# Turns of statistics, operand sums, attention loads and filter taps in a two-block transformer layer on one core

## The chip, the core and the metric

One core of a Trainium2 chip runs the whole program in one launch. The metric is the device time of one execution in microseconds. Every time below comes from one profiled execution of the kernel before, or from the unprofiled runs where that is said.

## The reference, cut to what matters

Two layers follow each other on 1,024 positions of width 1,024, in float32.

```python
# first block
h = rms_norm(x, norm_g);  u = h @ w_in
v_c, b_c, c_c, z_c, q, k, v, z_a, gate_logits = split(u)
y_a = (b_c * conv3(c_c * v_c) * silu(z_c)) @ w_conv_out
q, k = rms_norm(q) , rms_norm(k)                 # per head of 64
o   = window_attention(q, k, v, sinks) * silu(z_a)   # 16 heads, window 128
y_b = o @ w_attn_out
x   = x + (sigmoid(g_a) * y_a + sigmoid(g_b) * y_b) @ w_out
# second block
x = x + mixer(rms_norm(x)) ; x = x + cross_attention(rms_norm(x), mem)
u = rms_norm(x) @ w_up                           # 2 * 2816 columns
u = conv_b + w0 * u[t-2] + w1 * u[t-1] + w2 * u[t]
x = x + (silu(u[:, :2816]) * u[:, 2816:]) @ w_down
```

## The kernel before, in words

Activations lie with features on the 128 partitions and positions along the row. The 1,024 positions are two halves of 512 (`h` 0 and 1); a width of 1,024 is eight tiles (`kt`). A float32 product is made from three matmuls on high and low parts: ScalarE copies the high part, VectorE (sometimes GpSimd) subtracts it to get the low part. A **dense** page (`dense`, lines 381 to 383 for its matmuls) is 24 matmuls of 128x512 for one half. A **pair** of pages (`wino`, matmuls at lines 410 to 412) covers two pages and both halves with seven products of 12 matmuls instead of eight. Its operands besides the pages are the halves themselves and four sums of halves, T1 to T4, which `sums` (lines 447 to 487) makes from normalised tiles: subtractions in place, then a high and a low part for each of four tiles. T1 is wanted in the second product of the first pair, T2 in the third, T3 in the fifth, T4 in the seventh.

Everything else is woven between matmuls by hand. `tick()` is one **turn**: it sends the pending low parts of weights, one step of the pair being prepared, and one step of every generator in `side`. A dense page calls it halfway and at its end, a pair after every product. Each engine runs its instructions in the order in which they were written, so what a turn emits sits behind all that was emitted earlier on that engine. Loads and stores issued on `nc.sync` go through SyncE's queue (SP), those on `nc.gpsimd` through GpSimd's, also each in written order. Small tiles come from rings: 64 half tiles (`hp`), 8 temporaries (`tp`), two raw weight pages (`wr`), and a region reopened from stage to stage (`pg`, `hq`).

The places that the change touches:

- `x_thread` (lines 687 to 703) normalises one half. Each of eight tiles is written to a temporary, split into high and low, and stored to memory (`hraw`).
- `hT_sums` (lines 835 to 855) waits until both halves are normalised and the keys and values are stored, reopens the region, loads all 16 stored tiles back in three turns and a side generator, and then runs `sums`. Meanwhile TensorE works through four dense `z` pages; then come two `z` pairs, four `q` pairs, four `gb` pairs, eight times two convolution pairs and four `ga` pairs.
- `q_out` (lines 863 to 891) evacuates each quarter of a `q` pair: a square, a high and a low part. Its `stats`, run in the next turn, stores the two parts, sums the squares over each head with four small matmuls (line 882) and raises the mean to a power on GpSimd.
- `att_in` (lines 1022 to 1038) issues on GpSimd all loads of one group of heads and one half: two of keys, eight of queries, four of `z`, and for the first group two of values. Both groups of half 0 are issued before the convolution output pages `co` begin; the others are issued at units 9 and 17.
- `attention` (line 1155 on) takes 32 units, one a turn, after three empty turns, alongside `co`. In a turn come the values of three units ago, the finish and transpose of earlier ones (lines 1103 and 1123), and the scores of the new unit (line 1073), whose masked tile `pr` is first filled by GpSimd (line 1066) in the four units that have no block before them.
- `Up` (line 1728 on) evacuates an up page of the feed-forward layer: a copy to `u`, the last tap and the bias as a scaled copy on ScalarE, then two taps on VectorE (lines 1746 and 1747), all in the same turn. The first three of 22 page couples are plain dense pages, and `sums` for the other 19 runs beside them.

Of the kernel before, what the change touches and what calls it, by code (L numbers as in the profile page):

```python
# [17 lines left out]
HT = 512  # L18
# [98 lines left out]
def _body(es, tc, nc, wp, vec, xT, memT, gk2, pw, cst, out, dbg):  # L117
# [328 lines left out]
    def sums(t, X, hts):  # L446


        at = {"T1": (0, 0), "T2": (4, 1), "T3": (0, 1), "T4": (4, 0)}
        his, los = {}, {}  # L450

        def u(name, k):
            return t[at[name][0] + k, at[name][1]]

        def hi(name, k):
            his[name, k] = hts[name](name, F32R)
            S.copy(his[name, k], u(name, k))

        def lo(name, k):
            los[name, k] = hts[name](name, F32R)  # L460
            V.tensor_tensor(los[name, k], u(name, k), f(his[name, k]), ALU.subtract)  # L461
            if k == 3:
                X[name] = [(his[name, i], los[name, i]) for i in range(4)]

        for k in range(4):
            V.tensor_tensor(u("T1", k), u("T3", k), u("T1", k), ALU.subtract)
            V.tensor_tensor(u("T3", k), u("T3", k), u("T2", k), ALU.subtract)
            hi("T1", k)
            yield
        for k in range(4):  # L470
            V.tensor_tensor(u("T2", k), u("T2", k), u("T1", k), ALU.subtract)
            lo("T1", k)
            hi("T2", k)
            yield
        for k in range(4):
            lo("T2", k)
            V.tensor_tensor(u("T4", k), u("T4", k), u("T2", k), ALU.subtract)
            hi("T3", k)
            yield
        for k in range(4):  # L480
            lo("T3", k)
            hi("T4", k)
            if k:
                lo("T4", k - 1)
            yield
        lo("T4", 3)
# [184 lines left out]
    hraw = {}  # L671
# [15 lines left out]
    def x_thread(h):  # L687
# [7 lines left out]
        for kt in range(KT):  # L695
            t = tp("xn")
            V.scalar_tensor_tensor(t, xs[kt][h], col("norm_g", kt), R, ALU.mult, ALU.mult)
            hT[kt][h] = [None, None]
            sp.add(t, hT[kt][h], "xn")
            hraw[kt, h] = dram("hraw")  # L700
            nc.sync.dma_start(hraw[kt, h], t)
            if kt % 2:
                yield
# [130 lines left out]

    def hT_sums():
        while None in [x[1] for x in hT] or len(kd) < 8 or len(vd) < 4:
            yield
        reopen("q1pool", 16)
        t = {}
        order = [(kt, h) for k in range(4) for kt, h in ((k, 0), (k, 1), (k + 4, 1))] + [(k, 0) for k in range(4, 8)]  # L840

        def loads():
            for i, (kt, h) in enumerate(order):
                t[kt, h] = (hp if (kt < 4) == (h == 0) or kt == 7 else hq)("ht")
                nc.sync.dma_start(t[kt, h], hraw[kt, h])
                if i in (3, 7, 9, 11, 13):
                    yield

        g = loads()
        for _ in range(3):  # L850
            next(g)
            yield
        side.append(g)
        yield from sums(t, XB, {"T1": hp, "T2": hp, "T3": hq, "T4": hq})

# [10 lines left out]
    def q_out(p, j, h, o):  # L866
# [10 lines left out]
        def stats():  # L877
            for dst, src in zip(qd[p, j, h], (qh, ql)):
                nc.sync.dma_start(dst, f(src))
# [8 lines left out]
            return  # L888
            yield
# [132 lines left out]
    def att_in(p, h):  # L1022

        if h == 0:
            kp[p] = pg("kh", F32R), pg("kl", F32R)
        for i in range(2):
            nc.gpsimd.dma_start(f(kp[p][i][:, h * HT:(h + 1) * HT]), kd[p, h, i])
        for j in range(4):
            qT[p, j, h] = hp("qh", F32R), hp("ql", F32R)
            for i in range(2):  # L1030
                nc.gpsimd.dma_start(f(qT[p, j, h][i]), qd[p, j, h][i])
            if j == 1 and p == 0:
                vv[h] = pg("vh", F32R, (P, 4, 256)), pg("vl", F32R, (P, 4, 256))
                for i in range(2):
                    nc.gpsimd.dma_start(f(vv[h][i]), vd[h, i])
        for j in range(4):
            oT[p][j][h] = hp("o")
            nc.gpsimd.dma_start(oT[p][j][h], zd[p, j, h])

    class Unit:  # L1040
# [17 lines left out]
        def scores(self):  # L1058
# [6 lines left out]
            if n == 0:  # L1065
                G.memset(pr, -1e30)
# [87 lines left out]
    def attention():  # L1154
# [4 lines left out]
        for _ in range(3):  # L1159
            yield  # L1160
        for i in range(n + 3):
# [15 lines left out]
            if i in (9, 17):  # L1177
                att_in(i // 16, 1)
# [19 lines left out]
    for p in range(2):  # L1198
        att_in(p, 0)
    gate_in(gin, gad, 0, 0)  # L1200
    while None in [yc[c][0] for c in range(KT)]:
# [524 lines left out]
    class Up:  # L1726
# [5 lines left out]
        def tile(self, w, h):  # L1732
            u = self.u[w, h] = tp("u", shape=(P, HT + 2))
            if h == 0:
                G.memset(u[:, 0:2], 0.0)  # L1735
            return u[:, 2:]

        def conv(self, w, h):
            base = (NFF if w else 0) + self.ft
            w0, w1, w2 = (col("ffn_w", k * 44 + base) for k in range(3))  # L1740
# [4 lines left out]
            S.activation(a, u[:, 2:], AF.Identity, bias=col("ffn_b", base), scale=w2)  # L1745
            V.scalar_tensor_tensor(a, u[:, 1:HT + 1], w1, a, ALU.mult, ALU.add)  # L1746
# [11 lines left out]
        def plain(self, w):  # L1758
            def run(o, h):
                S.copy(self.tile(w, h), o)  # L1760
                self.conv(w, h)
                if w == 0:
                    side.append(self.gate_later(h))
                else:
                    self.out(h)
            return run

        def gate_later(self, h):
            yield
            self.gate(h)  # L1770
# [269 lines left out]
```

## Time and profile before

| What | us |
|---|---|
| unprofiled runs: median of 3 (lowest to highest) | 2487.8 (2484.42 to 2496.45) |
| profiled execution, its own time | 2496.53 |
| its span, first to last instruction | 2494.7 |
| TensorE busy in the span | 2394.4 |
| VectorE / ScalarE / GpSimd busy | 1471.7 / 1010.2 / 608.5 |

Busy time of an engine is the sum of its instructions without overlap; the span less that is the time in which the engine had nothing running. The profiled execution's time is 1.8 us above its span. [...]

### The profile page before, as it was taken

The numbers are of one execution on the slowest core, as the hardware profiler recorded it, in microseconds if no ns is written. First come the engines' busy times: TensorE is split into PE (matmuls) and PEld (weight loads), VectorE is DVE, ScalarE is ACT, GpSimd is POOL, SyncE is SP. The second block draws the span as 40 slices with busy tenths as digits, with TensorE's granted clock in tenths as the row PEclk, the third lists the DMA queues.
The fourth block names the chain that finished last, engine by engine and source line by source line (L and its number), as shares of the span: only waits on it lengthen the run. The fifth ranks groups of instructions, "written<-read, shape, count | busy, mean of one in ns | idle before, by whom it ended". The sixth has DMA issues, their size and how long they took to land. (4 is left out here: it accounts for less than half of the span.)

```text
span 2494.7 us, 30966 instructions
## 1 busy us (share of the span) xinstructions
PE 2394.4 (96%) x11550; PEld 1959.4 (79%) x11550; DVE 1471.7 (59%) x2303; ACT 1010.2 (40%) x1871; POOL 608.5 (24%) x629
## 2 busy tenths in 40 slices
PE   8988899999997889999999999999999999999998
PEld 7866688888885677887887888888878888878887
DVE  6642336666634778646435556455677878874335
ACT  5433343333343666334512334344455555562212
POOL 3234432333313555022001020001204233310003
PEclk9999999999998999999999999999999999999999
DMA  4622231211246533641100235322522222244322
GB/s 164 249 93 102 102 110 60 80 65 68 68 136 231 190 133 104 211 145 61 51 28 28 76 115 165 120 70 89 169 65 80 81 96 77 76 140 151 101 78 89
DMA packets 106231, 269.17 MB, mean 108 GB/s; under 512 B 12352, under 2 KB 14816, under 8 KB 106080
## 3 DMA queue, kind: packets, MB, share of 16 engines
q1 hardware_dynamic: 98544, 244.11, 29.1%
q0 software_dynamic: 6992, 22.55, 2.5%
q8 instruction: 91, 1.49, 0.2%
q10 hardware_dynamic: 544, 0.52, 0.1%
q14 instruction: 60, 0.49, 0.1%
HBM read 205.28 MB, written 61.87 MB: 107 GB/s over the span
## 5 line engine op out<-in xcount | busy, mean ns | idle before, releaser
L411 PE MATMUL pss<-T,wsh 128*128 128x512 f32 x588 | 232.4, 395 | 9.2 <-DVE T L461 9.2
L410 PE MATMUL pss<-T,wsh 128*128 128x512 f32 x588 | 236.6, 402 | 2.0 <-DVE cb L991 1.2
L345 DVE TENSOR_TENSOR wl<-wr,wh 128x1024 fp32r<-128x1024 f32 (+1 forms) x147 | 177.3, 1206 | 99.2 <-ACT wh L281 99.1
L412 PE MATMUL pss<-T,wsl 128*128 128x512 f32 x588 | 232.6, 396 | 0.0
L566 POOL TENSOR_TENSOR sq<-sq,sq 128x512 f32<-128x512 f32 (+1 forms) x58 | 70.9, 1223 | 610.2 <-ACT sq L562 609.1
L298 POOL TENSOR_TENSOR ws<-wr 128x512 f32<-128x512 f32 x49 | 70.8, 1445 | 586.4 <-DMA wr<-in_wp_dram 468.3
L330 DVE TENSOR_TENSOR wsl<-ws,wsh 128x512 fp32r<-128x512 f32 x196 | 188.1, 1000 | 33.4 <-ACT wsh L312 32.4
L281 ACT CAST wh<-wr 128x1024 fp32r<-128x1024 f32 (+1 forms) x147 | 148.2, 1008 | 143.0 <-PE psmm L382 133.1
L381 PE MATMUL psmm<-xnh,wh 128*128 128x512 f32 x448 | 179.5, 401 | 3.0 <-ACT wh L281 3.0
L383 PE MATMUL psmm<-xnh,wl 128*128 128x512 f32 x448 | 176.0, 393 | 1.3 <-DVE wl L345 1.3
L382 PE MATMUL psmm<-xnl,wh 128*128 128x512 f32 x448 | 176.0, 393 | 1.1 <-POOL u L1735 0.8
L412 PE MATMUL psmm<-xnh,wl 128*128 128x512 f32 x392 | 154.0, 393 | 1.6 <-DVE wl L302 1.6
L410 PE MATMUL psmm<-xnh,wh 128*128 128x512 f32 x392 | 154.6, 394 | 0.0
L411 PE MATMUL psmm<-xnl,wh 128*128 128x512 f32 x392 | 153.4, 391 | 0.0
L411 PEld LDWEIGHTS pss<-T,wsh 128*128 128x128 f32 x588 | 112.2, 191 | 34.1 <-DVE T L461 10.5
L410 PEld LDWEIGHTS pss<-T,wsh 128*128 128x128 f32 x588 | 111.9, 190 | 32.0 <-ACT pss L417 5.1
L412 PEld LDWEIGHTS pss<-T,wsl 128*128 128x128 f32 x588 | 112.0, 191 | 25.8
L383 PE MATMUL psmm<-fh,wl 128*128 128x512 f32 (+1 forms) x300 | 116.0, 387 | 1.1 <-DVE wl L345 1.1
L381 PE MATMUL psmm<-fh,wh 128*128 128x512 f32 (+1 forms) x300 | 116.0, 387 | 0.0
L382 PE MATMUL psmm<-fl,wh 128*128 128x512 f32 (+1 forms) x300 | 115.9, 386 | 0.0
L562 ACT ACTIVATE sq<-x 128x512 f32<-128x512 f32 (+1 forms) x80 | 47.1, 588 | 165.3 <-DVE x L1255 110.5
L302 DVE TENSOR_TENSOR wl<-wr,wh 128x1024 fp32r<-128x1024 f32 x49 | 60.9, 1243 | 85.9 <-ACT wh L296 85.9
(453 smaller groups left out, 6288.9 us busy)
## 6 DMA issues: line engine op xcount, KB each, us to landing
wr<-in_wp_dram SPq DMA_DIRECT2D x238, 512.0 KB, 3.7
act<-fa SPq DMA_DIRECT2D x44, 256.0 KB, 2.0
fr<-act SPq DMA_DIRECT2D x44, 256.0 KB, 4.6
wr<-in_wp_dram SPq DMA_DIRECT2D x24, 384.0 KB, 3.2
xd<-x SPq DMA_DIRECT2D x32, 256.0 KB, 4.4
x<-xd SPq DMA_DIRECT2D x32, 256.0 KB, 4.0
x<-in_xT_dram SPq DMA_DIRECT2D x16, 256.0 KB, 5.7
hraw<-xn SPq DMA_DIRECT2D x16, 256.0 KB, 2.3
```

Of the source, the lines that this page charges most:

```text
L281: S.copy(hi[:, :n], raw[:, :n])
L298: G.tensor_tensor(sg[0], a21, a22, ALU.add)
L302: V.tensor_tensor(l12, r1, f(h12), ALU.subtract)
L330: V.tensor_tensor(lo, raw, f(hi), ALU.subtract)
L345: V.tensor_tensor(lo, raw, f(hi), ALU.subtract)
L381: T.matmul(out_ap, lh, rh, start=first, stop=False)
L382: T.matmul(out_ap, lh, rl, start=False, stop=False)
L383: T.matmul(out_ap, ll, rh, start=False, stop=last)
L410: T.matmul(o, lh, rh, start=first and kt == 0, stop=False, skip_group_check=True)
L411: T.matmul(o, lh, rl, start=False, stop=False, skip_group_check=True)
L412: T.matmul(o, ll, rh, start=False, stop=kt == 3, skip_group_check=True)
L566: eng.tensor_tensor(self.acc, self.acc, sq, ALU.add)
```

## The change

Six edits, none of which alters what is computed:

1. `sums` takes 18 turns instead of 17. In a turn it first makes the low part of the tile whose high part came a turn ago, then the high part of the tile subtracted a turn ago, then the new subtractions.
2. The second half is normalised in place (`xs[kt][1]`) and neither stored nor loaded back. Half 0's first four tiles are loaded ahead of the wait in `hT_sums`, the other four in a side generator, and `sums` begins in the turn in which the wait ends.
3. `stats` of a query quarter begins one turn later.
4. Attention loads go out on SyncE, two a turn, three steps ahead of `co` and the others from `side`; the second half's from units 8 and 16 on. Attention has four empty turns in place of three.
5. The fill of `pr` is VectorE's.
6. In the plain up pages the two taps come a turn after the scaled copy and the gate or product a turn after that; the small fill of `u` there is VectorE's.

```diff
@@ -447,6 +447,7 @@
         at = {"T1": (0, 0), "T2": (4, 1), "T3": (0, 1), "T4": (4, 0)}
+        order = ("T1", "T2", "T3", "T4")
         his, los = {}, {}
@@ -462,28 +463,22 @@
...
-        for k in range(4):
-            V.tensor_tensor(u("T1", k), u("T3", k), u("T1", k), ALU.subtract)
-            V.tensor_tensor(u("T3", k), u("T3", k), u("T2", k), ALU.subtract)
-            hi("T1", k)
-            yield
-        for k in range(4):
-            V.tensor_tensor(u("T2", k), u("T2", k), u("T1", k), ALU.subtract)
-            lo("T1", k)
-            hi("T2", k)
-            yield
-        for k in range(4):
-            lo("T2", k)
-            V.tensor_tensor(u("T4", k), u("T4", k), u("T2", k), ALU.subtract)
-            hi("T3", k)
-            yield
-        for k in range(4):
-            lo("T3", k)
-            hi("T4", k)
-            if k:
-                lo("T4", k - 1)
-            yield
-        lo("T4", 3)
+        for i in range(18):
+            if 2 <= i and i - 2 < 16:
+                j = i - 2
+                lo(order[j // 4], j % 4)
+            if 1 <= i < 17:
+                j = i - 1
+                hi(order[j // 4], j % 4)
+            k = i % 4
+            if i < 4:
+                V.tensor_tensor(u("T1", k), u("T3", k), u("T1", k), ALU.subtract)
+                V.tensor_tensor(u("T3", k), u("T3", k), u("T2", k), ALU.subtract)
+            elif i < 8:
+                V.tensor_tensor(u("T2", k), u("T2", k), u("T1", k), ALU.subtract)
+            elif i < 12:
+                V.tensor_tensor(u("T4", k), u("T4", k), u("T2", k), ALU.subtract)
+            yield
@@ -668,7 +663,7 @@
     hR, hT = grid(KT), grid(KT)
-    hraw = {}
+    hraw, ht = {}, {}
     nrms = [Norm(), Norm()]
@@ -693,12 +688,15 @@
...
         for kt in range(KT):
-            t = tp("xn")
+            t = xs[kt][h] if h else tp("xn")
             V.scalar_tensor_tensor(t, xs[kt][h], col("norm_g", kt), R, ALU.mult, ALU.mult)
...
             sp.add(t, hT[kt][h], "xn")
-            hraw[kt, h] = dram("hraw")
-            nc.sync.dma_start(hraw[kt, h], t)
+            if h:
+                ht[kt, h] = t
+            else:
+                hraw[kt] = dram("hraw")
+                nc.sync.dma_start(hraw[kt], t)
             if kt % 2:
@@ -832,27 +830,25 @@
...
+    def ht_in(kt, pool):
+        ht[kt, 0] = pool("ht")
+        nc.sync.dma_start(ht[kt, 0], hraw[kt])
+
     def hT_sums():
+        for k in range(4):
+            ht_in(k, hp)
+            if k % 2:
+                yield
         while None in [x[1] for x in hT] or len(kd) < 8 or len(vd) < 4:
...
         reopen("q1pool", 16)
-        t = {}
-        order = [(kt, h) for k in range(4) for kt, h in ((k, 0), (k, 1), (k + 4, 1))] + [(k, 0) for k in range(4, 8)]
-
-        def loads():
-            for i, (kt, h) in enumerate(order):
-                t[kt, h] = (hp if (kt < 4) == (h == 0) or kt == 7 else hq)("ht")
-                nc.sync.dma_start(t[kt, h], hraw[kt, h])
-                if i in (3, 7, 9, 11, 13):
-                    yield
-
-        g = loads()
-        for _ in range(3):
-            next(g)
-            yield
-        side.append(g)
-        yield from sums(t, XB, {"T1": hp, "T2": hp, "T3": hq, "T4": hq})
-
+        side.append(ht_rest())
+        yield from sums(ht, XB, {"T1": hp, "T2": hp, "T3": hq, "T4": hq})
+
+    def ht_rest():
+        for k in range(4, 8):
+            ht_in(k, hp if k == 7 else hq)
+            yield
@@ -875,6 +871,7 @@
...
         def stats():
+            yield
             for dst, src in zip(qd[p, j, h], (qh, ql)):
@@ -885,8 +882,6 @@
...
                             mhalf.rearrange("p (a b) -> p a b", b=2), ALU.pow)
-            return
-            yield
@@ -1021,21 +1016,27 @@
...
+        def two(a, b):
+            for dst, src in zip(a, b):
+                nc.sync.dma_start(dst, src)
+
         if h == 0:
             kp[p] = pg("kh", F32R), pg("kl", F32R)
-        for i in range(2):
-            nc.gpsimd.dma_start(f(kp[p][i][:, h * HT:(h + 1) * HT]), kd[p, h, i])
+        two([f(t[:, h * HT:(h + 1) * HT]) for t in kp[p]], [kd[p, h, i] for i in range(2)])
+        yield
         for j in range(4):
             qT[p, j, h] = hp("qh", F32R), hp("ql", F32R)
-            for i in range(2):
-                nc.gpsimd.dma_start(f(qT[p, j, h][i]), qd[p, j, h][i])
+            two([f(t) for t in qT[p, j, h]], qd[p, j, h])
+            yield
             if j == 1 and p == 0:
                 vv[h] = pg("vh", F32R, (P, 4, 256)), pg("vl", F32R, (P, 4, 256))
-                for i in range(2):
-                    nc.gpsimd.dma_start(f(vv[h][i]), vd[h, i])
-        for j in range(4):
-            oT[p][j][h] = hp("o")
-            nc.gpsimd.dma_start(oT[p][j][h], zd[p, j, h])
+                two([f(t) for t in vv[h]], [vd[h, i] for i in range(2)])
+                yield
+        for j in range(0, 4, 2):
+            for i in (j, j + 1):
+                oT[p][i][h] = hp("o")
+            two([oT[p][i][h] for i in (j, j + 1)], [zd[p, i, h] for i in (j, j + 1)])
+            yield
@@ -1063,7 +1064,7 @@
...
             if n == 0:
-                G.memset(pr, -1e30)
+                V.memset(pr, -1e30)
             s = [ps("s", (P, 2, 256)) for _ in range(2)]
@@ -1156,7 +1157,7 @@
...
         dv = None
-        for _ in range(3):
+        for _ in range(4):
             yield
@@ -1174,8 +1175,8 @@
...
                 units[i].scores()
-            if i in (9, 17):
-                att_in(i // 16, 1)
+            if i in (8, 16):
+                side.append(att_in(i // 16, 1))
             if todo:
@@ -1195,9 +1196,16 @@
...
-    for p in range(2):
-        att_in(p, 0)
     gate_in(gin, gad, 0, 0)
+    first = att_in(0, 0)
+    for _ in range(3):
+        next(first)
+
+    def rest():
+        yield from first
+        yield from att_in(1, 0)
+
+    side.append(rest())
     while None in [yc[c][0] for c in range(KT)]:
@@ -1729,20 +1737,29 @@
...
-        def tile(self, w, h):
+        def tile(self, w, h, eng=G):
             u = self.u[w, h] = tp("u", shape=(P, HT + 2))
             if h == 0:
-                G.memset(u[:, 0:2], 0.0)
+                eng.memset(u[:, 0:2], 0.0)
             return u[:, 2:]
         def conv(self, w, h):
+            self.tap2(w, h)
+            self.taps(w, h)
+
+        def tap2(self, w, h):
             base = (NFF if w else 0) + self.ft
-            w0, w1, w2 = (col("ffn_w", k * 44 + base) for k in range(3))
+            w2 = col("ffn_w", 2 * 44 + base)
             u = self.u[w, h]
...
             S.activation(a, u[:, 2:], AF.Identity, bias=col("ffn_b", base), scale=w2)
+
+        def taps(self, w, h):
+            base = (NFF if w else 0) + self.ft
+            w0, w1 = (col("ffn_w", k * 44 + base) for k in range(2))
+            u, a = self.u[w, h], self.a[w, h]
             V.scalar_tensor_tensor(a, u[:, 1:HT + 1], w1, a, ALU.mult, ALU.add)
@@ -1757,17 +1774,19 @@
...
             def run(o, h):
-                S.copy(self.tile(w, h), o)
-                self.conv(w, h)
-                if w == 0:
-                    side.append(self.gate_later(h))
-                else:
-                    self.out(h)
+                S.copy(self.tile(w, h, V), o)
+                self.tap2(w, h)
+                side.append(self.later(w, h))
             return run
-        def gate_later(self, h):
-            yield
-            self.gate(h)
+        def later(self, w, h):
+            yield
+            self.taps(w, h)
+            yield
+            if w == 0:
+                self.gate(h)
+            else:
+                self.out(h)
```

## Rows read from the trace of the kernel before

**Rows 1.** The page: the span, and TensorE's busy time.
```profile
span 2494.7 us, 30966 instructions
...
PE 2394.4 (96%) x11550; PEld 1959.4 (79%) x11550; DVE 1471.7 (59%) x2303; ACT 1010.2 (40%) x1871; POOL 608.5 (24%) x629
```

**Rows 2.** TensorE's waits: line and tile, releaser, us in total, times, longest.
```profile
PE pst L882 <- ACT qsq L871: 17.9, 16, 1.5
PE pss L1073 <- DVE pr L1078: 13.3, 1, 13.3
PE pso L1146 <- ACT pch L1125: 9.3, 4, 6.5
PE pss L411 <- DVE T L461: 9.2, 3, 3.6
PE pst L1123 <- POOL pr L1103: 7.0, 1, 7.0
...
PE psmm L381 <- ACT wh L281: 3.0, 1, 3.0
```

**Rows 3.** Busy time by stretch (PE, PEld, DVE, ACT, POOL), clock, DMA: pairs.
```profile
119.70:153.00 33.30, 24.06 (x87) 18.56 (x86) 25.13 (x28) 12.91 (x23) 14.68 (x8) 0.85 0.24 77
153.00:172.00 19.00, 19.00 (x85) 15.61 (x84) 7.01 (x8) 7.75 (x13) 6.00 (x4) 1.00 0.29 103
172.00:294.80 122.80, 104.90 (x466) 83.14 (x465) 35.74 (x63) 41.09 (x69) 44.02 (x27) 0.92 0.28 103
294.80:371.00 76.20, 76.20 (x335) 62.53 (x335) 28.40 (x34) 32.97 (x52) 32.11 (x22) 1.00 0.32 111
```

**Rows 4.** TensorE's instructions in order, query stage: start, duration, line, count, idle.
```profile
215.47 1.10 PE L882 MATMUL pst<-blk,qsq 128*128 128x64 f32 x8 [0.75 <-ACT qsq L871]
216.38 0.48 PE L410 MATMUL pss<-T,wsh 128*128 128x512 f32 x1
```

**Rows 5.** VectorE's instructions in order: the first subtraction of the sums.
```profile
97.61 0.69 DVE L466 TENSOR_TENSOR ht<-ht,ht 128x512 f32<-128x512 f32 x1 [7.45 <-DMA ht<-hraw]
```

**Rows 6.** GpSimd's instructions in order, start of attention and second loads.
```profile
757.75 0.63 POOL L1027 DMA_DIRECT2D kh<-kd  x1 [39.33 <-PE pss L412]
...
785.76 0.54 POOL L1066 MEMSET pr<- 128x512 f32 x1
...
853.53 2.04 POOL L1103 TENSOR_TENSOR pr<-pr,den 128x512 f32<-128x512 f32 x2
```

**Rows 7.** TensorE's instructions in order: second unit's scores, and two transposes.
```profile
786.83 0.81 PE L1073 MATMUL pss<-kh,qh 64*128 64x128 f32 x2 [13.30 <-DVE pr L1078]
...
916.03 0.60 PE L1123 MATMUL pst<-ident,pr 128*128 128x128 f32 x4
...
921.72 0.60 PE L1123 MATMUL pst<-ident,pr 128*128 128x128 f32 x4
```

**Rows 8.** Busy time by stretch, as rows 3: attention, then the plain up pages.
```profile
763.00:789.00 26.00, 12.70 (x67) 10.18 (x66) 5.04 (x10) 3.93 (x6) 12.20 (x23) 0.78 1.00 387
786.80:791.20 4.40, 4.37 (x18) 3.72 (x19) 2.96 (x8) 2.12 (x9) 0.05 (x1) 0.51 0.51 163
854.60:859.60 5.00, 4.96 (x22) 3.98 (x23) 2.42 (x6) 2.79 (x6) 2.29 (x4) 0.52 0.82 311
907.00:911.00 4.00, 3.95 (x12) 2.55 (x14) 3.83 (x9) 3.25 (x10) 2.21 (x4) 0.55 0.16 60
935.00:966.00 31.00, 31.00 (x183) 24.95 (x183) 27.55 (x78) 21.65 (x73) 18.63 (x30) 1.00 0.32 110
1790.00:1872.00 82.00, 74.53 (x319) 58.67 (x319) 63.99 (x92) 44.07 (x69) 12.89 (x15) 0.98 0.26 88
```

**Rows 9.** VectorE's instructions in order: low halves of reloaded conv tiles.
```profile
849.62 1.29 DVE L493 TENSOR_TENSOR ycl<-ycr,ych 128x512 fp32r<-128x512 f32 x2
```

**Rows 10.** The page's DMA issues: count, KB each, median us to landing.
```profile
wr<-in_wp_dram SPq DMA_DIRECT2D x238, 512.0 KB, 3.7
...
qdh<-qh SPq DMA_DIRECT2D x16, 256.0 KB, 2.0
```

## The prediction

> **What bounds the kernel now.** I read the page first: TensorE is busy 2394.4 of 2494.7 us [rows 1], so no other engine bounds the span as a whole and an edit that removes no matmul can give back at most the 100.3 us in which TensorE has nothing to do, and what it loses at its lower clock. Next TensorE's waits, longest in total first: five lines hold 56.7 of the 100 us [rows 2], and each lies in a place that the change touches: the query statistics (17.9), the masked fill of the first attention units (13.3), ScalarE's copy of turned probabilities (9.3, of which 6.5 once), the low parts of the operand sums (9.2) and GpSimd's finish of a unit (7.0). Then the busy time by stretch, which shows each stage's own limit. A pair with nothing in its way takes 19.0 us, and the four gate pairs after the queries take 76.2 us, all busy, at full clock [rows 3]. [...] The first pair takes 33.3 us with 9.2 idle and a clock of 0.85, 5.0 us more.
>
> **Query statistics a turn later.** Four small matmuls stand between two products and take 216.38 - 215.47 = 0.91 us [rows 4]; they stay, 16 times. What goes is their wait for ScalarE's square of the tile that the product before has only just finished, at most 1.5 us each [rows 2]. A turn later a whole product of 19.0 / 7 = 2.7 us [rows 3] lies between, so the square is long done. I book 17.9 + 9.8 = 27.7 us. Bounds: nothing, if the wait returns at the next evacuation, and 122.8 - 76.2 - 16 x 0.91 = 32.0 us. VectorE's small step on the sums and GpSimd's power move with the statistics and have a turn of slack. The two stores of a quarter move too, past whatever SP gets in the next turn; what is late then is the temporaries. The ring has eight, a quarter takes three or four, so a buffer is wanted again two turns later, 2 x (2.7 + 0.9) = 7.2 us. The store can start when the low part is made, at most two steps of ScalarE and two of VectorE after the product, some 0.7 us each like the subtraction in [rows 5], and takes 2.0 us to land [rows 10]: 7.2 - 2.8 - 2.0 = 2.4 us to spare, and none if SP is held for a turn.
>
> [...]
>
> **Operand sums.** Removed: eight stores and eight loads of 256 KB on SP; half of the rest moves ahead of the wait. The first subtraction waited 7.45 us for its load [rows 5]. Counting turns, the wait in the generator ends in the same turn as before; then T1 is complete after 6 turns instead of 3 + 8, T2 after 10 instead of 15, T3 after 14 instead of 19, T4 after 18 instead of 20. The first pair begins 11 turns after the wait, so T1 to T3 are there a turn or more early. T4's last low part is emitted in the very turn before its product and queues on VectorE behind that turn's evacuation and weights: three or four operations of 0.7 us against 2.3 us until the matmul that reads it, so up to 1.5 us. Booked: 9.2 + 5.0 - 1.5 = 12.7 us; bounds 5 (T4 late by a whole chain of low parts) and 14.2. The eight in-place tiles hold eight of the 64 half tiles up to 14 turns longer; I take their cost as nothing, since four of them free places in the region and T1's own tiles go back before the pair is prepared. If that cover fails, weight parts wait for buffers, at the price of the lost 12.7 us.
>
> **Attention.** The kernel before issues 32 loads on GpSimd in one go, from 757.75 us on [rows 6]. The fill of `pr` comes behind them at 785.76 us, VectorE behind the fill, and the second unit's scores start at 786.83 us after 13.3 us of waiting [rows 6, 7]. The second batch does the same to the finish at 853.53 us (7.0 us) and the third to a copy (6.5 us). After the change GpSimd has neither loads nor fill. Behind these three waits the clock stands at 0.51, 0.52 and 0.55 for 4.4, 5.0 and 4.0 us [rows 8], another 2.2 + 2.4 + 1.8 = 6.4 us. Together 13.3 + 7.0 + 6.5 + 6.4 = 33.2 us.
>
> What comes in its place: 60 loads on SP, two a turn. The first stretch is full: 387 GB/s at a DMA share of 1.00 from 763 to 789 us [rows 8]. Ahead of the second unit's last operand SP now has about 5.25 MB in order (6 head tiles, the values, 4 more, two pages, three gate tiles), which at that rate is 13.6 us from about 760 us, plus 2 us to land: 775.6. The unit comes a turn later than the 773.5 us at which it began to wait [rows 7], about 776: I take off 1 us. Four fills on VectorE cost 0.54 us each at most [rows 6]; the trace has none there, and four together are 2 us beside VectorE's work. That work is the next limit: 27.55 of 31.0 us [rows 8], or 5.1 us of each 5.7 us turn (two transposes lie 921.72 - 916.03 us apart [rows 7]). While the second half of the convolution output is reloaded, 1.29 us a turn more [rows 9] makes 6.3 us against 5.7, for about four turns, and splits of finished tiles fall in the same turns. I take off 3 us. The fourth empty turn moves one unit from `co` into the next stage, at no cost that I can see, since that stage has room. Booked 33.2 - 4 = 29.2 us; bounds 14 (the first wait returns in full with its clock, 15.5, beside the 4 us) and 33.2.
>
> [...]
>
> **Plain up pages.** From 1790 to 1872 us TensorE is idle 82.0 - 74.5 = 7.5 us and loses 0.02 x 82 = 1.6 us [rows 8]. The longest single wait, 3.0 us, is for ScalarE's copy of a page [rows 2], which sits behind a high part of the sums that waits for VectorE, which waits for ScalarE's scaled copy. With the taps a turn behind and the sums staggered, neither engine waits inside a turn. No operation is added; VectorE is busy 64 of 82 us, so the work fits. About half of the 9.1 us belongs to the norm ahead of it: I book 5, bounds 0 and 9.
>
> **Sum.** 27.7 + 12.7 + 29.2 + 5.0 = 74.6 us. The profiled execution took 2496.5 us (span and 1.8 us around it), so 2421.9 by its own measure. It stands 8.7 us above the median of the runs shown. Part of that difference may be stretches at half clock which the change removes anyway, so I take off about half: **2418 us**. All upper bounds together, 32.0 + 14.2 + 33.2 + 9, against the median give 2399.
>
> **Rivals.**
>
> - *SP becomes the wait at attention.* The pages of `co` queue behind head tiles, and SP itself may be held by a load whose buffer is not free. For: the full DMA stretch, and a page takes 3.7 us to land even at median load [rows 10]. Against: two loads a turn are 0.5 MB in 5.7 us, 92 GB/s of 387. The first wait of 13.3 us and some of its clock return, and pages come late in two or three turns more: about 25 us, 2443. Chance 0.09.
> - *The clock does not follow the waits.* If the half-speed stretches hang on something other than the short waits, 9.8 + 5.0 + 6.4 us stay: 2439. Against it stand the full-clock pairs on both sides of the query stage. Chance 0.05.
> - *The statistics' turn does not do what it says*: the temporaries' ring of eight holds each quarter until its stores land, evacuations slip, and the matmuls wait as before. Half of the 27.7 us stays: 2432. Chance 0.07.
> - *Slower than before.* Head tiles for the second half wait on SP for buffers that only attention's own units free, and the page behind them starts late each time. A page landing in 3.7 us with its copy and low part behind it (1 us each at least) is some 6 us exposed; over the 16 pages of `co` 96 us, so 2514. It decides when SP is held for longer than a page's lead of one dense half (24 matmuls, twice a product, 5.4 us) on nearly every page. Rows against it: a unit frees its queries as soon as its scores are made, a turn before the loads ask. Chance 0.03.
>
> **How the numbers follow.** The forecast has 0.76. Its own spread is 2398 to 2432 from the bounds of the terms; the first two rivals reach 2443, and I close at 2446, with the low end at 2398. That leaves out the slower case and tails on either side. A measurement of this kernel can tell about 0.5%, 12 us. Everything but the slower rival is below 2475: faster 0.96, same 0.02, slower 0.02 (a third of that rival would come out even).
>
> **What would show it.** In the changed kernel's trace line 882's successor has no wait for the square; four query pairs take about 92 us at clock 1.00; the first pair about 20 us with no wait for T2 or T3; the second unit's scores start near 776 us less what was gained earlier; no transposes wait for GpSimd; and the page copy in the plain up pages starts without a chain ahead of it. A query stage above 105 us, a wait for a page in `co`, or TensorE's idle time above 55 us would make the prediction wrong.

## The result and the profile after

The changed kernel takes 2412.1 us (median of 4 runs, 2409.3 to 2414.8) against 2488.1 beside it: a ratio of 0.969, 95% interval 0.966 to 0.972, 76 us less. The forecast was 2418 with a range of 2398 to 2446.

The page's first lines, against [rows 1]: 83.0 us of span went between the two profiled executions, 57.3 of them idle time of TensorE (100.3 to 43.0) and 25.7 busy time, most of it from stretches with a lower granted clock before (0.85 and 0.92 in [rows 3], 0.51 to 0.55 in [rows 8]; the mean over the span rose from 0.984 to 0.996).

```profile
span 2411.7 us, 30908 instructions
...
PE 2368.7 (98%) x11550; PEld 1947.3 (81%) x11550; DVE 1484.3 (62%) x2313; ACT 1009.0 (42%) x1871; POOL 576.2 (24%) x559
```

TensorE's waits, against [rows 2]: the wait for the query square is gone, those of attention and of the sums have shrunk to rests.

```profile
PE pso L1147 <- POOL pph L1134: 3.1, 7, 0.6
PE pss L411 <- DVE T L462: 2.4, 1, 2.4
...
PE psmm L383 <- DVE wl L345: 1.8, 2, 1.1
PE pss L1074 <- DMA qh<-qdh: 1.5, 1, 1.5
```

Busy time by stretch, against [rows 3] and [rows 8] (columns: stretch, its length, busy time of TensorE, its weight loads, VectorE, ScalarE and GpSimd, granted clock, DMA share, GB/s). The first two pairs take 42.71 us (33.30 + 19.00 before), the four query pairs 90.39 (122.8), and the plain up pages (the last row) are all busy. Around the second attention unit (715 to 755) 1.7 us are idle, at full clock; in the turns of the reload (785 to 821) VectorE is busy for 33.80 of 36.0 us, the limit that the prediction named.

```profile
120.45:163.16 42.71, 40.27 (x169) 32.58 (x168) 25.00 (x24) 19.11 (x34) 18.06 (x12) 0.96 0.27 93
163.16:253.55 90.39, 90.39 (x457) 76.42 (x456) 37.84 (x61) 40.57 (x70) 40.02 (x26) 1.00 0.38 137
715.00:755.00 40.00, 38.28 (x210) 30.67 (x209) 25.11 (x59) 20.45 (x57) 4.95 (x8) 1.00 0.80 294
785.00:821.00 36.00, 32.33 (x185) 23.12 (x185) 33.80 (x92) 23.07 (x79) 14.31 (x22) 1.00 0.53 180
1708.00:1784.00 76.00, 76.00 (x344) 63.13 (x343) 64.26 (x95) 43.87 (x67) 16.19 (x11) 1.00 0.30 103
```

The table below does this for every kernel of the study. It cuts each profiled execution at the start of five matmuls that all kernels have: the first pair, the first query pair, the first `gb` pair, the first norm statistic behind attention (line 568 after the change), and line 444 in the feed-forward layer. What lies ahead of the first pair moved by 4.4 us from execution to execution (117.3 to 121.7) and is left out.

| kernel | median us | two pairs | query pairs | `gb` to norm | norm to L444 | rest |
|---|---|---|---|---|---|---|
| before | 2488.1 | 52.2 | 122.7 | 825.4 | 745.3 | 629.2 |
| after | 2412.1 | 42.7 | 90.4 | 795.1 | 736.4 | 626.7 |
| after_again | 2411.5 | 41.1 | 90.4 | 795.3 | 736.2 | 627.1 |
| u_stats | 2442.8 | 41.1 | 121.1 | 793.5 | 736.0 | 627.2 |
| u_order | 2411.3 | 38.4 | 90.4 | 797.3 | 737.7 | 626.7 |
| u_loads | 2417.6 | 46.7 | 90.4 | 794.6 | 736.0 | 626.8 |
| u_att | 2443.1 | 41.1 | 90.4 | 827.4 | 736.1 | 627.1 |
| u_taps | 2416.4 | 41.1 | 90.4 | 796.1 | 739.8 | 627.6 |
| u_three | 2430.0 | 53.5 | 90.3 | 795.3 | 746.6 | 627.6 |
| att_vfill | 2437.1 | 42.8 | 90.4 | 819.7 | 736.3 | 626.3 |
| sp_burst | 2430.7 | 41.1 | 90.4 | 812.5 | 736.1 | 626.8 |
| pool_paced | 2414.9 | 41.1 | 90.4 | 800.5 | 736.5 | 626.3 |
| stats_half | 2418.7 | 41.1 | 96.1 | 794.6 | 737.6 | 626.7 |
| trim | 2406.4 | 38.4 | 90.4 | 794.1 | 736.0 | 626.2 |

From before to after the stages give 9.5 + 32.3 + 30.3 + 8.9 + 2.5 = 83.5 us. How far a stage's length can be read: eight kernels have the same attention code (after, after_again, u_stats, u_order, u_loads, u_taps, u_three, stats_half), and their `gb` to norm stage lies between 793.5 and 797.3 us. The theory that the experiments test is the prediction's own: four separate gains, one for each of these places.

### The profile page after: what moved, and what is told of

The parts are those of the page before. It is cut to its first block, busy times and chain, and to the rows that moved or that the text cites. A ratio compares the mean times of both kernels' runs of the same rounds, so it can differ in the third digit from the quotient of the medians.

```text
span 2411.7 us, 30908 instructions
## 1 busy us (share of the span) xinstructions
PE 2368.7 (98%) x11550; PEld 1947.3 (81%) x11550; DVE 1484.3 (62%) x2313; ACT 1009.0 (42%) x1871; POOL 576.2 (24%) x559
## 3 DMA queue, kind: packets, MB, share of 16 engines
q8 instruction: 91, 1.49, 0.3%
## 4 chain that ended last, share of the span: by engine, by line
PE 82%; DVE 9%; ACT 6%; issue 2%; DMA 1%; POOL 1%; SPq 0%; DVEq 0%; POOLq 0%; ACTq 0%
PE psmm L381 13%; PE psmm L383 13%; PE psmm L382 13%; PE pss L410 5%; PE pss L412 5%; PE pss L411 5%; PE psmm L410 4%; PE psmm L412 4%; PE psmm L411 3%; ACT pr L1096 2%; PE pst L410 2%; PE pst L412 2%; PE pst L411 2%; PE pso L410 2%; PE pso L412 2%
## 5 line engine op out<-in xcount | busy, mean ns | idle before, releaser
L410 PE MATMUL pss<-T,wsh 128*128 128x512 f32 x588 | 233.6, 397 | 2.4 <-DVE cb L986 1.2
L411 PE MATMUL pss<-T,wsh 128*128 128x512 f32 x588 | 229.7, 391 | 2.4 <-DVE T L462 2.4
L330 DVE TENSOR_TENSOR wsl<-ws,wsh 128x512 fp32r<-128x512 f32 x196 | 194.9, 1035 | 34.3 <-ACT wsh L312 32.4
```

The lines of the kernel that those rows point to most:

```text
L330: V.tensor_tensor(lo, raw, f(hi), ALU.subtract)
L410: T.matmul(o, lh, rh, start=first and kt == 0, stop=False, skip_group_check=True)
L411: T.matmul(o, lh, rl, start=False, stop=False, skip_group_check=True)
```

## The experiments

Each kernel is the changed one with the edit shown, so an undone part reads as what it is worth. Differences are taken from 2412.1 us, and for u_three, stats_half and trim from the changed kernel itself, run again beside them:

> The changed kernel itself, once more, beside the trimmed one. It tells how far two measurements of one program lie apart: 2410 to 2414 us, a profile whose stages differ from the first one's by under 2 us in all.

Measured 2411.5 us (2410.7 to 2412.6), so two measurements of one program lie 0.6 us apart. Its first two pairs took 41.1 us and not 42.7, though the same wait of 2.44 us stands in them: in the first profile the clock fell behind that wait (0.72 from 141 to 147 us), here it stayed at 1.00.

**u_stats: the statistics back in their own turn.**

```diff
         def stats():
-            yield
             for dst, src in zip(qd[p, j, h], (qh, ql)):
...
```

> The changed kernel with the query statistics back in the turn right after the evacuation. Theory (each part's gain lies in its own stage): the query stage goes from 90.6 us back to about 122 us, with some 18 us of waits for the square and a granted clock near 0.92; the rest of the trace keeps its lengths within 1 us; the time is 2412 + 31 = 2443 us. Rival (the waits were already hidden behind something else that the other edits removed): the stage stays below 105 us.

Measured 2442.8 us, ratio to before 0.981 (0.980 to 0.983), 30.6 above the changed kernel, as the theory had it. The query stage is as before in clock and waits and within 1.6 us of its length; the other stages move by 1.6 us at most. First the window, then three of the sixteen waits in TensorE's timeline (columns: start, duration, engine, line, operation, output and inputs, shapes; in brackets the idle time before it and what ended it):

```profile
162.79:283.88 121.09, 103.17 (x466) 81.70 (x464) 35.72 (x63) 41.09 (x69) 44.00 (x27) 0.93 0.29 104
```

```profile
264.32 1.10 PE L878 MATMUL pst<-blk,qsq 128*128 128x64 f32 x8 [0.75 <-ACT qsq L867]
269.74 1.10 PE L878 MATMUL pst<-blk,qsq 128*128 128x64 f32 x8 [1.50 <-ACT qsq L867]
276.73 1.10 PE L878 MATMUL pst<-blk,qsq 128*128 128x64 f32 x8 [1.50 <-ACT qsq L867]
```

**stats_half: only the even tiles' statistics a turn later.** Does the clock follow these waits?

```diff
         def stats():
-            yield
+            if j % 2 == 0:
+                yield
```

> The statistics of the odd query tiles are formed in their own turn as before, those of the even ones a turn later. Eight of the sixteen waits come back, 17.9 / 2 = 9.0 us. Theory (the granted clock falls with these waits, and in proportion): half of the 9.8 us that the clock cost as well, less some 1.5 us that the later start of attention gives back, so 2412 + 12 = 2424 us and a granted clock of about 0.95 to 0.97 over the query pairs. Rival (the clock only falls when each turn has its wait): the waits alone, 2412 + 9 - 1.5 = 2419.5 us at a clock of 1.00.

Measured 2418.7 us, near the rival, but by another count: only four waits came back, one for each pair, 3.8 us in all. In the other odd turns two groups of statistics, the late one and the prompt one, stand together, and the wait shrinks away.

```profile
162.47:258.59 96.12, 92.34 (x465) 77.90 (x464) 36.62 (x62) 41.12 (x69) 41.81 (x26) 1.00 0.37 132
```

```profile
178.18 1.10 PE L880 MATMUL pst<-blk,qsq 128*128 128x64 f32 x8 [1.02 <-ACT qsq L867]
...
202.21 1.10 PE L880 MATMUL pst<-blk,qsq 128*128 128x64 f32 x8 [0.92 <-ACT qsq L867]
```

One wait of about 1 us in 24 us left the clock at 1.00 here. The stage is 5.7 us longer: 3.8 are waits, 0.8 is the last group of statistics, which falls into the stage again, and the rest is small change, mainly groups that take 0.9 to 1.0 us instead of 0.81 beside a wait or another group.

**u_order and u_loads: the two halves of the sums edit, each undone alone.** u_order has the old order of steps in `sums` with the new loads; u_loads has the old stores, loads and start with the new order.

```diff
 # u_order
-        for i in range(18):
...
+        for k in range(4):
+            lo("T3", k)
+            hi("T4", k)
+            if k:
+                lo("T4", k - 1)
+            yield
+        lo("T4", 3)
 # u_loads
-            t = xs[kt][h] if h else tp("xn")
+            t = tp("xn")
...
+        for _ in range(3):
+            next(g)
+            yield
...
```

> The changed kernel with the old order of steps in the operand sums (high part in the turn of its subtraction, 17 turns), loads as changed. Theory (the sums start three turns sooner, and that is the gain at the first pair): first two pairs within 3 us of the changed kernel's 42.9 us, and the plain up pages lose half of their 9 us, since there the chain of subtraction, high part and low part inside one turn returns: 2412 + 6 = 2418 us. Rival (the order inside a turn is the gain at the first pair): those two pairs go back to about 52 us, and the time to 2425 us or more.

> The changed kernel with both halves stored and loaded back as before and the sums starting three turns after the wait, the new order kept. Theory (the early start is the gain at the first pair): T3 and T4 are late by a turn or more, the first two pairs take 50 us or more instead of 42.9, nothing else moves: 2412 + 8 = 2420 us. Rival (the order inside a turn is the gain): 42.9 us within 2, 2413 us.

u_order measured 2411.3 us (2410.2 to 2411.9): beside the new loads the new step order gives nothing, and both expected times miss. Of the theory the first half holds, the pairs don't go back; the loss in the up pages is 1.3 us where 6 were expected. With the old order the two pairs are all busy; the later stages take back what it gave (797.3 and 737.7 in the table).

```profile
118.58:156.98 38.40, 38.40 (x169) 31.54 (x168) 23.77 (x26) 18.64 (x33) 18.10 (x12) 1.00 0.30 104
```

u_loads measured 2417.6 us (2415.6 to 2420.4), 5.5 above, all of it in the two pairs (5.3 us of waits for low parts), and between its theory and its rival. So the new order doesn't make up for the old loads; how much of the 12.7 us booked the loads give is told only by a kernel with both undone (u_three, below).

**u_taps: the taps in the turn of the scaled copy.**

```diff
-                S.copy(self.tile(w, h, V), o)
-                self.tap2(w, h)
-                side.append(self.later(w, h))
+                S.copy(self.tile(w, h), o)
+                self.conv(w, h)
...
```

> The changed kernel with the taps of the plain up pages back in the turn of the scaled copy and the small fill on GpSimd. Theory (taps a turn behind remove VectorE's wait for ScalarE inside a turn): the stretch from 1708 us to the first pair of the feed-forward layer loses 4 to 9 us, about half of what the changed kernel gained there, the order of the sums keeping the other half: 2412 + 5 = 2417 us. Rival (the order of the sums does it all): within 1.5 us of the changed kernel.

Measured 2416.4 us (2414.0 to 2417.9), 4.2 above: a hit on its theory. But the stages that it stands in had given 8.9 + 2.5 = 11.4 us. Parts undone singly were short of the whole in two places, so all three went into one kernel.

**u_three: order, loads and taps all as before.** The diffs are the three above.

> Step order of the sums, the loads of the second halves with their two transfers, and the taps are all three as before; the query statistics and the attention loads are as changed. Theory (the three cover for one another: a wait that one of them leaves open is filled while the other stands): the two stages take what they took before, the first two pairs 52.1 us where the changed kernel has 42.9, and from the norm to the gated stage's end 10.7 us more than the changed kernel, so 2412 + 9 + 11 = 2432 us. Rival (the parts add up): -0.8 (order), +5.5 (loads) and +4.2 (taps) as each gave alone, so 2421 us.

Measured 2430.0 us (2428.8 to 2433.3), 18.4 above: the parts cover for one another. In the two pairs, new loads alone bring 53.5 us down to 38.4 (u_order) and the new order alone to 46.7 (u_loads), so the loads suffice, and the order is worth something only without them. The two pairs are back at 53.5 us with the waits of [rows 2] to a tenth, and so is the wait for ScalarE's copy of a page.

```profile
PE pss L411 <- DVE T L461: 9.3, 3, 3.7
...
PE psmm L381 <- ACT wh L281: 3.0, 1, 3.0
```

The timelines show that second wait: VectorE and ScalarE of u_three, then ScalarE of the changed kernel. In u_three VectorE's tap waits 1.86 us for the scaled copy, the subtraction stands behind the taps, the high part of the sum waits 2.93 us for the subtraction, and the page's copy `wh` stands behind the high part. In the changed kernel the high part's subtraction was made a turn earlier, and the copy follows without idle time.

```profile
1763.70 0.75 DVE L1758 SCALAR_TENSOR_TENSOR fa<-u,vt,fa 128x512 f32<-128x512 f32 x1 [1.86 <-ACT fa L1757]
...
1765.88 0.68 DVE L471 TENSOR_TENSOR ft<-ft,ft 128x512 f32<-128x512 f32 x1
```

```profile
1766.60 0.62 ACT L457 CAST T<-ft 128x512 fp32r<-128x512 f32 x1 [2.93 <-DVE ft L471]
1767.12 1.04 ACT L281 CAST wh<-wr 128x1024 fp32r<-128x1024 f32 x1
```

```profile
1766.04 0.60 ACT L458 CAST T<-ft 128x512 fp32r<-128x512 f32 x1
1766.55 1.05 ACT L281 CAST wh<-wr 128x1024 fp32r<-128x1024 f32 x1
```

Either edit cuts this chain, late taps because VectorE no longer waits inside a turn, late high parts because ScalarE doesn't; with one in place the other is worth 1.3 to 4.3 us in the last two columns of the table.

**u_att: loads in bursts on GpSimd, the fill on GpSimd, three empty turns.**

```diff
-            two([f(t) for t in qT[p, j, h]], qd[p, j, h])
-            yield
+            for i in range(2):
+                nc.gpsimd.dma_start(f(qT[p, j, h][i]), qd[p, j, h][i])
...
-                V.memset(pr, -1e30)
+                G.memset(pr, -1e30)
...
-            if i in (8, 16):
-                side.append(att_in(i // 16, 1))
+            if i in (9, 17):
+                att_in(i // 16, 1)
...
```

> The changed kernel with attention loads in bursts on GpSimd, the fill on GpSimd and three empty turns. Theory: the three waits of 13, 7 and 6.5 us return with their lower clock, and the stretch from the first convolution output page to the norm behind the first projection grows from 372.7 us to 404 us: 2412 + 31 = 2443 us. Rival (part of the gain came from the earlier stages' better supply): less than 20 us return.

Measured 2443.1 us, ratio to before 0.981 (0.980 to 0.983), 31.0 above, as the theory had it. The three waits of [rows 2] are back.

```profile
PE pss L1068 <- DVE pr L1073: 14.0, 1, 14.0
PE pso L1141 <- ACT pch L1120: 8.2, 4, 5.9
PE pst L1118 <- POOL pr L1098: 6.9, 1, 6.9
```

GpSimd issues from 712.99 us on and reaches the fill at 741.21; VectorE's masked copy behind it has waited 15.32 us.

```profile
712.99 0.63 POOL L1022 DMA_DIRECT2D kh<-kd  x1 [39.19 <-PE pss L411]
...
728.74 0.54 POOL L1033 DMA_DIRECT2D o<-zd  x1 [2.82 <-DMA vl<-vd]
...
741.21 0.54 POOL L1061 MEMSET pr<- 128x512 f32 x1
```

```profile
741.78 0.44 DVE L1073 COPY_PREDICATED pr<-iC,pss 128x256 f32<-128x256 uint8 x1 [15.32 <-POOL pr L1061]
```

The next three kernels ask which of its traits does the harm.

**att_vfill: as u_att, but the fill on VectorE.** The edit is shown against u_att.

```diff
-                G.memset(pr, -1e30)
+                V.memset(pr, -1e30)
```

> The changed kernel with attention loads in bursts on GpSimd and three empty turns, but the fill on VectorE. Theory (the waits come from what stands behind the loads in GpSimd's order, one instruction each): the wait of 13 us at the second unit is gone but for the landing of its queries (under 2 us), those of 7.0 and 6.5 us for the finish behind the second and third bursts return: some 17 us above the changed kernel with their clock, 2429 us. Rival (the loads themselves are late, whoever fills): 13 us or more of waiting at the second unit remain, 2440 us.

Measured 2437.1 us (2435.7 to 2438.4), 25 above and between theory and rival. The second unit now waits for its loads alone, 1.49 us and three times less (731.83). But the finish, GpSimd's next work behind the same burst, waits in the fill's place (746.09), a second finish and a copy behind the later bursts (806.35, 857.91).

```profile
731.83 0.33 PE L1068 MATMUL pss<-kh,qh 64*128 64x128 f32 x2 [1.49 <-DMA qh<-qdh]
...
746.09 1.12 PE L1118 MATMUL pst<-ident,pr 128*128 128x128 f32 x4 [6.26 <-POOL pr L1098]
806.35 1.11 PE L1118 MATMUL pst<-ident,pr 128*128 128x128 f32 x4 [8.44 <-POOL pr L1098]
...
857.91 0.79 PE L1141 MATMUL pso<-pch,vh 128*128 128x512 f32 x1 [5.58 <-ACT pch L1120]
```

**sp_burst: the same bursts on SP.**

```diff
...
-    first = att_in(0, 0)
-    for _ in range(3):
-        next(first)
...
+    for p in range(2):
+        for _ in att_in(p, 0):
+            pass
```

> The changed kernel with its attention loads on SP, but in bursts: all of half 0 ahead of the first convolution output page, the others at once at units 8 and 16. [...] Rival (only GpSimd's order mattered, pacing is free): 2412 us within 3.

Measured 2430.7 us (2429.6 to 2431.9), 18.6 above, where the rival had it within 3. GpSimd is free of the loads, and TensorE still waits 14.86 us at the second unit, by another chain: the burst holds SP for 21 us, so the next page of `co` and the next gate tile are issued at 740 us (that page at 723.11 in the changed kernel), and ScalarE and VectorE stand for 22 us before the scores' own steps. TensorE, SP, ScalarE and VectorE:

```profile
749.75 0.47 PE L1074 MATMUL pss<-kh,qh 64*128 64x128 f32 x1 [14.86 <-DVE pr L1079]
```

```profile
701.33 0.38 SPq L241 DMA_DIRECT2D wr<-in_wp_dram  x1
...
740.12 0.33 SPq L241 DMA_DIRECT2D wr<-in_wp_dram  x1
740.74 0.32 SPq L1198 DMA_DIRECT2D g<-gad  x1
```

```profile
746.12 1.04 ACT L281 CAST wh<-wr 128x1024 fp32r<-128x1024 f32 x1 [22.26 <-DMA wr<-in_wp_dram]
```

```profile
746.78 0.69 DVE L1217 TENSOR_TENSOR g<-g,psmm 128x512 f32<-128x512 f32 x1 [21.67 <-DMA g<-gad]
```

**pool_paced: two a turn, but on GpSimd.**

```diff
             for dst, src in zip(a, b):
-                nc.sync.dma_start(dst, src)
+                nc.gpsimd.dma_start(dst, src)
```

> The changed kernel with its attention loads in the same turns, two a turn, but issued on GpSimd. Theory (the burst was the harm, not the engine): two issues of 0.54 us stand ahead of GpSimd's work in a turn, which has some 2.5 us of it in 5.7 us: 0 to 6 us above the changed kernel, 2412 to 2418 us. Rival (any load on GpSimd holds up the units): 1 us in each of 32 turns, 2440 us.

Measured 2414.9 us (2414.0 to 2415.9), 3 above, with a stage 5 us longer. So of the 31 us that u_att gave back, the pace is most: 18.6 us on SP (sp_burst), 22 on GpSimd (att_vfill, which has three empty turns besides). The engine that fills `pr` is worth 6 beside bursts, the engine that issues paced loads about 3. The pace is one of written order, not of time: GpSimd has nothing between the first 18 loads and issues them in one go here too, from 713 to 732 us. But its first finish stands behind 18 loads and not behind 30, and it waits for its input, not for a load.

```profile
731.71 0.54 POOL L1021 DMA_DIRECT2D kl<-kd  x1 [0.75 <-DMA ql<-qdl]
735.68 1.04 POOL L1104 TENSOR_TENSOR pr<-pr,den 128x512 f32<-128x512 f32 x1 [3.43 <-DVE den L1103]
```

**trim: three rests taken away.** The sums' tail two to a turn, the values' loads behind the queries, the reload of the second half one tile a turn and earlier.

```diff
-        for i in range(18):
+        turns = {i: (i - 1,) for i in range(1, 12)}
+        turns.update({12: (11, 12), 13: (13, 14), 14: (15,)})
+        for i in range(16):
...
-            if j == 1 and p == 0:
+            if j == 3 and p == 0:
                 vv[h] = ...
...
-            if h == 0 and m == 4:
-                side.append(reload([...], "yc", 2))
+            if h == 0 and m == 2:
+                side.append(reload([...], "yc", 2, 1))
```

> The changed kernel with three small edits: the last four operand sums are split two to a turn once the subtractions are done (16 turns in place of 18), the attention values are loaded behind all four query tiles in place of between them, and the reload of the second half's products starts two pages earlier with one tile a turn in place of two. Theory (the three places where the trace of the changed kernel still shows TensorE waiting): 2.4 us of the operand wait with up to 1.7 us of clock, about 1.5 of the 1.7 us at the second unit, and 2 to 3.5 us in the turns where VectorE is full: 2412 - 7 = 2405 us (2402 to 2408). Rival (VectorE's work only moves, and the same waits stand in other turns): 2410 to 2413 us.

Measured 2406.4 us (2405.0 to 2407.4), 5.1 below the changed kernel run beside it, with no overlap of the two sets of runs: the fastest version of the study, 0.966 of before (0.965 to 0.968). The sums give 2.7 us (38.4 against 41.1). In attention the wait of the second unit is gone (2.1 us in after_again), but the turns around 795 us keep 1.9 of some 3.2 us and 0.7 us of new waits stand ahead of them, much as the rival had it. The stage is 1.2 us shorter, less than it differs between kernels with one and the same attention code, so no share of the 5.1 us is shown for it.

```profile
791.32 0.50 PE L1147 MATMUL pso<-pcl,vh 128*128 128x512 f32 x1 [0.33 <-DVE pcl L1127]
796.85 0.47 PE L1147 MATMUL pso<-pch,vh 128*128 128x512 f32 x1 [0.54 <-ACT pr L1078]
```

## Why the prediction was right, and where a step was not

**Query statistics, booked 27.7, measured 32.3 in the stage and 30.6 when undone.** The mechanism held: no wait, four pairs at full clock in 90.4 us where some 92 were forecast. The clock was the mis-sized term. Of the 32.3 us, 17.9 are the waits, 0.9 is the last group of statistics, which now runs behind the stage and is no gain, and about 1.5 that a group with no wait beside it takes 0.81 us instead of the booked 0.91. That leaves 12 for the clock by subtraction (10.4 by the same count in u_stats), where 9.8 was booked. No run shows that 9.8 by itself: it is an estimate, 0.08 x 122.8 from the mean clock of 0.92 in [rows 3]. That the clock's share would go with the waits was my estimate too, and u_stats bears it out: put back alone, sixteen waits of at most 1.5 us bring a clock of 0.93 with them, and without them it is 1.00.

**Operand sums, booked 12.7, measured 9.5 (11.1 in the repeated profile).** The waits for T1 to T3 are gone, as forecast, and the new loads alone suffice for that (u_order against u_three). The step that failed is "T4's last low part ... up to 1.5 us": it cost 2.44 us, and in the first profile a stretch at a lower clock (0.72) besides. TensorE, VectorE and GpSimd there:

```profile
141.78 0.50 PE L411 MATMUL pss<-T,wsh 128*128 128x512 f32 x1 [2.44 <-DVE T L462]
```

```profile
134.90 1.28 DVE L330 TENSOR_TENSOR wsl<-ws,wsh 128x512 fp32r<-128x512 f32 x2
136.10 0.69 DVE L462 TENSOR_TENSOR T<-ht,T 128x512 fp32r<-128x512 f32 x1
...
137.67 2.38 DVE L330 TENSOR_TENSOR wsl<-ws,wsh 128x512 fp32r<-128x512 f32 x2
139.98 1.74 DVE L462 TENSOR_TENSOR T<-ht,T 128x512 fp32r<-128x512 f32 x1
```

```profile
137.83 1.68 POOL L298 TENSOR_TENSOR ws<-wr 128x512 f32<-128x512 f32 x1 [10.39 <-DVE c L902]
139.59 1.59 POOL L299 TENSOR_TENSOR ws<-ws,wr 128x512 f32<-128x512 f32 x1
```

I had counted three or four operations of 0.7 us; beside GpSimd's additions of weight parts these three take 1.2, 1.2 and 1.74 us. A turn earlier, with GpSimd idle, the same two subtractions took 1.28 us together instead of 2.38, and T4's low part would have taken 0.69: at those lengths the wait would have been about 0.3 us (an estimate from these rows). The 1.74 us operation starts inside an addition that ends at 141.18 us and itself ends at 141.72, 0.54 us later, somewhat less than the 0.69 us that such an operation took at 136.10 us with GpSimd idle. What makes it longer the trace doesn't name. The new order also put T4 a turn later than the old one would have: with the new loads the old order has no wait there at all (u_order), and 16 turns instead of 18 have none either (trim).

**Attention, booked 29.2, measured 30.3 in the stage and 31.0 when undone.** The mechanism holds: the chain through GpSimd is shown by u_att and att_vfill, the rest at the second unit is 1.7 us (1 booked), the idle time in the turns of the reload 3.7 us (3 booked). By these rests 27.8 us were due; the 2.5 more are no larger than the stage's own spread. The prediction's "32 loads in one go" are 30 in the trace, 16 and 14 for the two groups, which changes no term. The first rival's mechanism is real, only the change does not set it off: with bursts SP is the wait (14.86 us on TensorE in sp_burst), with two loads a turn no wait for a page is left in this stage. In the trace of sp_burst SP itself comes to the page's issue only at 740.12 us, and the 6 us from there to ScalarE's copy of the page at 746.12 are the smaller part of the 22.26 us that ScalarE waits. Whether the loads ahead of the page lengthen those 6 us no run here shows.

**Plain up pages, booked 5, measured 8.9, and 2.5 in the rest.** The step that failed is "about half of the 9.1 us belongs to the norm ahead of it": in [rows 8]'s stretch of the kernel before, at most 1.1 of the 7.5 us idle lie at the norm's last tiles (up to 1808.56 us), and 2.2 in the first pair behind line 444, whose gain I had not booked. Both are gone now.

```profile
1806.09 0.50 PE L382 MATMUL psmm<-xnl,wh 128*128 128x512 f32 x1 [0.34 <-POOL xnl L605]
1808.56 0.51 PE L382 MATMUL psmm<-xnl,wh 128*128 128x512 f32 x1 [0.77 <-POOL u L1735]
...
1867.95 0.50 PE L412 MATMUL psmm<-xnh,wl 128*128 128x512 f32 x1 [1.56 <-DVE wl L302]
1871.60 0.50 PE L412 MATMUL pst<-T,wsl 128*128 128x512 f32 x1 [0.59 <-DVE wsl L330]
```

Undone together with the order, the taps are worth 11 us in the last two columns (u_three), above the bound of 9; but only 0.9 of that lies in the rest, so for the other 1.6 of its 2.5 us no run gives a cause. The chain was the right one (u_three shows it link by link), but two edits cut it, so neither could be priced by itself.

**The sum.** 74.6 booked, 76 measured on medians and 83.0 between the profiled executions, where that of before stood 8.7 us above its median, which the forecast allowed for by half. By stages three terms ran over, by 4.6, 1.1 and 6.4 us, and one under, by 3.2, so 83.5 us stand against the 74.6. That the 76 on medians come so near to 74.6 is in part luck: terms that were too small in sum met a profiled execution that was slower than the median.

## What to carry to other kernels

Issue prefetches at the pace at which they are used: 30 loads in one go held whichever engine issued them for 21 to 28 us here, and everything behind them in order, while two a turn left some 2 us of waiting, with about 3 us between the two queues. Where an in-order engine waits in the middle of a turn, move the waiting step a turn later than its input, and look for two such steps on one chain before pricing either: undone singly, three edits gave -0.8, 5.5 and 4.2 us, together 18.4. Price a step that runs beside another engine's work by its slowest row, not by its usual one.

## What the runs showed that I had not expected

In these runs the granted clock did not go by the length of a wait alone. With sixteen waits of at most 1.5 us, one in 7.6 us on the mean, it was 0.93 over 121 us (u_stats); with four of about 1 us, 24 us apart, 1.00 (stats_half); behind one of 2.44 us it was 0.72 for 6 us in one execution of the changed kernel (after) and 1.00 in another (after_again). What decides in that last case stays open.

GpSimd issued a load in 0.54 us (u_att), so 30 are 16 us; the burst held it for 28, since behind the tenth or so most issues also waited, by the trace for an earlier load to land, up to 2.82 us. SP took 21 us for 30, though most of its issues took 0.3 to 0.5 us; what its gaps wait for the trace doesn't name.
